# A decoder trunk in split fp32: in each weight tile, the products with the residual weights are moved behind all products with the rounded weights

## The chip, the cores and the metric

The kernel runs on one core of one Trainium2 chip. The metric is the device time of one execution in microseconds (us), as the median over several runs.

## The reference

Two decoder layers over 256 tokens of width 2048. Each layer has a token mixer (layer 0: forgetting attention "fox" with 16 heads of 128; layer 1: sliding-window attention "swa" with 32 query and 4 key heads of 64 and partial rotary) and a gated ConvFFN of width 5632. Everything is float32:

```python
for i in range(DEPTH):
    mod = c_act @ ada_w[i] + ada_b[i]            # six vectors of 2048 for this layer
    sh1, sc1, g1, sh2, sc2, g2 = jnp.split(mod[:, None, :], 6, axis=-1)
    h = x * (1.0 + sc1) + sh1
    y = fox_attention(h, ...) if i % 2 == 0 else swa_attention(h, positions, ...)
    x = layer_norm(DEEPNORM_ALPHA * x + (1.0 + g1) * y, ln_mix_g[i], ln_mix_b[i])
    h = x * (1.0 + sc2) + sh2
    y = conv_ffn(h, ...)                         # u = h @ w_up; conv of width 3; (silu(g) * val) @ w_down
    x = layer_norm(DEEPNORM_ALPHA * x + (1.0 + g2) * y, ln_ffn_g[i], ln_ffn_b[i])
```

## The kernel before

**Split products.** A float32 product is made of three matmuls in the type fp32r. Each operand is a rounded part (named H or h) and a residual, that is the operand less its rounded part (named L or l). Of the four products, residual times residual is left out. So each piece of weights costs rounded weights times rounded activations, rounded weights times residual activations, and residual weights times rounded activations.

**Weight tiles.** Weights pass through the chip once, in 728 tiles of 128 x 2 x 512 floats (two row blocks of 128, 512 columns, 512 KB). `stream` handles one tile: SP issues the DMA into `w` (a pool of 10 buffers that the tiles `wa` of the adaLN weights share), ScalarE (ACT) casts it to `wh` (line 259), VectorE (DVE) subtracts to get `wl` (line 270, called the residual cast below), and then TensorE (PE) runs the products. There are 4 buffers of `wh` and 4 of `wl`; a buffer is free when its last product has run.

**Two product loops.** `w_mm` keeps the weights stationary: 8 cells per tile (2 row blocks `i`, 4 column blocks `f`), each with a 128 x 256 output `ws`, two outputs to a PSUM bank; 24 matmuls a tile, 416 tiles (fox q and k, and both FFN up-projections). `x_mm` keeps the activations stationary and moves 512 weight columns: 4 cells (2 token halves `t`, 2 row blocks), outputs `xs` of one bank each; 12 matmuls a tile, 312 tiles (fox v, the swa input, both output projections, both FFN down-projections). `x_mm_end` is used for the last tiles of a stage: first all of them for `t=0`, then for `t=1`.

**Other work on the same engines.** The six adaLN vectors per layer are made on DVE in the background (`acc`, line 385, one instruction per 512 KB tile `wa`), at a rate per weight tile that is set stage by stage; in the opening (0 to about 174 us) the first two are made from tiles `wo` (`oacc`, lines 516 and 518) with PE sums `cps`. Attention heads run in steps between weight tiles: PE scores `S`, DVE and ACT softmax (`pr`, lines 633, 637, 645), PE transposes `T`, ACT copy `pT` (line 659), PE output `o`. `residual` (lines 561, 563, 565, 568) adds a finished stage to `x` and takes the LayerNorm moments, which GpSimd (POOL) turns into `rs`; then `normalise` (584, 586) and the transposes of `x` (463) make the next stage's `hH` and `hL`.

**What sets the order.** The program calls these in the order of the loops, but a scheduler of the framework orders the instructions of each engine from its own estimate of when operands are ready; instructions marked by `pin(..., True)` keep the program's order. Each engine then runs its list strictly in that order.

Of the kernel before, what the change touches and what calls it, by code (L numbers as in the profile page):

```python
# [17 lines left out]
P = 128  # L18
# [23 lines left out]
def hybrid_trunk(ctx: ExitStack, tc: tile.TileContext, a: dict, out: bass.AP):  # L42
# [32 lines left out]
    def mm(o, lhsT, rhs, start=False, stop=False, **kw):  # L75
        return nc.tensor.matmul(o, lhsT, rhs, start=start, stop=stop, **kw)  # L76
# [202 lines left out]
    def x_mm(ps, kc, h, l, stat, last, first=0, ts=range(NT)):  # L279

        for t in ts:
            for i in range(2):
                xh, xl = stat(kc + i, t)
                mm(ps[t], xh, h[:, i, :], start=kc + i == first)
                mm(ps[t], xh, l[:, i, :])
                mm(ps[t], xl, h[:, i, :], stop=kc + i == last)

    def x_mm_end(ps, stat, nk, n):

        kept = []  # L290

        def use(kc, h, l):
            end = kc >= nk - 2 * n
            x_mm(ps, kc, h, l, stat, nk - 1, ts=(0,) if end else range(NT))
            if end:
                kept.append((kc, h, l))
            if kc + 2 >= nk:
                for e in kept:
                    x_mm(ps, *e, stat, nk - 1, ts=(1,))

        return use

    def w_mm(ps, kc, h, l, last=KC - 1, first=0):

        for i in range(2):
            for f in range(4):
                o = ps[f // 2][:, f % 2, :]
                wh, wl = h[:, i, f * P:(f + 1) * P], l[:, i, f * P:(f + 1) * P]
                mm(o, wh, hH[:, kc + i, :], start=kc + i == first and f % 2 == 0, skip_group_check=True)
                mm(o, wh, hL[:, kc + i, :], skip_group_check=True)  # L310
                mm(o, wl, hH[:, kc + i, :], stop=kc + i == last, skip_group_check=True)

    def x_stationary(wsrc, col, k0, nk, stat, end=0):

        ps = x_banks()
        use = x_mm_end(ps, stat, nk, end) if end else lambda kc, h, l: x_mm(ps, kc, h, l, stat, nk - 1)
        stream(wsrc, k0, col, list(range(nk)), use)
        return ps

    def w_stationary(wsrc, col):  # L320

        ps = w_banks()
        stream(wsrc, 0, col, list(range(KC)), lambda kc, h, l: w_mm(ps, kc, h, l))
        return ps
# [127 lines left out]
    hH = cst.tile([P, KC, S], F32R, name="hH")  # L452
    hL = cst.tile([P, KC, S], F32R, name="hL")
# [248 lines left out]
    def fox(l, j):  # L702
# [118 lines left out]
        def first_block(blk, k2, part):  # L821
            if part == 0 and blk not in banks:
                def change():
                    for b, ps in banks.items():
                        if b not in old:
                            old[b] = []
                            for i, p in enumerate(ps):
                                g = [f32(gtile("part")).rearrange("p a b -> p (a b)") for _ in range(2)]
                                for gi, pi in zip(g, p):
                                    nc.scalar.copy(gi, pi if i == 2 else pi.rearrange("p a s -> p (a s)"))  # L830
                                old[b].append(g)
                    banks[blk] = w_banks(), w_banks(), x_banks()

                then(change)
            k = 2 * k2

            def use(kc, h, l):
                if part < 2:
                    w_mm(banks[blk][part], kc, h, l, last[blk])
                else:  # L840
                    x_mm(banks[blk][part], kc, h, l, hstat, last[blk])

            stream(w_in, 0, part * FW + blk * WB, [k, k + 1], use)
            done[blk] = k + 2
# [4 lines left out]
        for blk, rate in zip((1,0,2,3), (.9,1.1,1.2,1.4)):  # L849
            then(lambda rate=rate: ada.update(rate=rate))  # L850
            q, k, V = [], [], []
            n = done.get(blk, 0)

            def more(part, banks_, mul):
                if n == KC:
                    return banks[blk][part]
                ps = banks_()
                stream(w_in, 0, part * FW + blk * WB, list(range(n, KC)), lambda kc, h, l: mul(ps, kc, h, l, n))
                return ps

            o = old.get(blk, [None] * 3)
            wm = lambda ps, kc, h, l, n: w_mm(ps, kc, h, l, first=n)
            pq = more(0, w_banks, wm)
            then(lambda ps=pq, q=q, o=o: defer(evac_qk(ps, 0, q, o[0])))
            pk = more(1, w_banks, wm)
            then(lambda ps=pk, k=k, o=o: defer(evac_qk(ps, 1, k, o[1])))
            pv = more(2, x_banks, lambda ps, kc, h, l, n: x_mm(ps, kc, h, l, hstat, KC - 1, first=n))
            then(lambda ps=pv, V=V, o=o, hs=[head(blk, hh, q, k, V) for hh in range(4)]: defer(evac_v(ps, V, hs, o[2])))
# [229 lines left out]
```

## Time and profile before

| what | value |
|---|---|
| median of 3 runs | 2311.9 us (2309.21 to 2316.67) |
| profiled execution: span, the only time the page gives of it | 2317.4 us |
| PE busy / weight loads (PEld) busy | 97% / 89% |
| DVE / ACT busy | 78% / 49% |
| DMA, mean | 258 GB/s |
| residual casts, line 270 | 728, 1221 ns each |
| casts to rounded, line 259 | 728, 1051 ns each |
| adaLN accumulations, line 385 | 308, 1276 ns each |

The span runs from the first to the last instruction of one profiled execution. It is 5.5 us above the median of the runs, inside 0.3%. Ends of matmuls are modelled, so a busy PE only says that matmuls follow each other; their pace is read from how many start in a stretch. PEld is the weight load that precedes each matmul.

### The profile page before, as it was taken

Reading aid. Unit: us, or ns where it says so; the run is one execution under the profiler, and the core shown is the slowest. Engines: PE = TensorE matmul, PEld = TensorE weight load, DVE = VectorE, ACT = ScalarE, POOL = GpSimd, SP = SyncE. Lnnn points to the kernel's source line nnn. Section 1 sums busy time; section 2 is a strip of 40 time slices with the busy share of each in tenths; the row PEclk is TensorE's granted clock in tenths of the full one; section 3 lists DMA queues with packets and bytes.
Section 4 is the critical chain, followed back from the end, with each engine's and each line's share of the span. In section 5 each row is a group of like instructions: output and inputs, shape, how many; then the busy total and the mean of one; then the engine's idle time right before and its main releaser. Section 6 shows DMA issues by size and latency. Waiting matters only on the chain.

```text
span 2317.4 us, 38661 instructions
## 1 busy us (share of the span) xinstructions
PE 2243.1 (97%) x15061; PEld 2060.3 (89%) x15061; DVE 1804.0 (78%) x2609; ACT 1135.8 (49%) x1685; POOL 40.7 (2%) x79
## 2 busy tenths in 40 slices
PE   6899999999999999999999999999999999999997
PEld 5899998789999988999987778779999988999986
DVE  7788978879977876887887998899878655666655
ACT  1335654445555433454543478745555533454532
POOL 1001000010000000000001000000000000000000
PEclk9899999999999999999999999999999999999999
DMA  9998989968887897887897685778888566666663
GB/s 331 308 338 274 349 326 345 326 220 303 300 266 236 286 313 261 288 285 238 292 303 255 211 303 190 232 282 280 262 262 255 178 192 195 186 189 185 187 192 111
DMA packets 285561, 598.86 MB, mean 258 GB/s; under 512 B 20790, under 2 KB 53816, under 8 KB 285376
## 3 DMA queue, kind: packets, MB, share of 16 engines
q1 hardware_dynamic: 284768, 595.85, 78.1%
q8 instruction: 118, 1.93, 0.3%
q0 software_dynamic: 608, 0.53, 0.1%
q14 instruction: 67, 0.55, 0.1%
HBM read 594.21 MB, written 2.10 MB: 257 GB/s over the span
## 4 chain that ended last, share of the span: by engine, by line
PE 84%; DVE 10%; ACT 3%; issue 2%; DMA 1%; POOL 0%; SPq 0%; DVEq 0%; POOLq 0%; ACTq 0%
PE ws L76 49%; PE xs L76 30%; DVE wl L270 2%; DVE acc L385 2%; PE sm L76 1%; ACT wh L259 1%; PE cps L76 1%; PE o L76 1%; DVE oacc L518 1%; PE S L76 1%; PE sm L463 1%; ACT pr L645 0%; ACT pr L637 0%; PE T L657 0%; DVE x L563 0%
## 5 line engine op out<-in xcount | busy, mean ns | idle before, releaser
L270 DVE TENSOR_TENSOR wl<-w,wh 128x1024 fp32r<-128x1024 f32 x728 | 888.0, 1221 | 407.0 <-ACT wh L259 386.3
L259 ACT CAST wh<-w 128x1024 fp32r<-128x1024 f32 x728 | 762.9, 1051 | 864.6 <-PE ws L76 323.2
L76 PE MATMUL ws<-hH,wh 128*128 128x256 f32 x3328 | 945.8, 285 | 6.0 <-ACT wh L259 6.0
L76 PE MATMUL ws<-hH,wl 128*128 128x256 f32 x3328 | 936.9, 282 | 4.3 <-DVE wl L270 4.2
L76 PE MATMUL ws<-hL,wh 128*128 128x256 f32 x3328 | 939.5, 283 | 0.2 <-DVE hL L86 0.2
L76 PEld LDWEIGHTS ws<-hH,wh 128*128 128x128 f32 x3328 | 634.4, 191 | 10.0 <-ACT wh L259 6.8
L76 PEld LDWEIGHTS ws<-hH,wl 128*128 128x128 f32 x3328 | 637.2, 192 | 5.7 <-DVE wl L270 5.7
L76 PEld LDWEIGHTS ws<-hL,wh 128*128 128x128 f32 x3328 | 633.5, 190 | 2.7 <-issue 1.9
L76 PE MATMUL xs<-wh,gT 128*128 128x512 f32 x1408 | 437.2, 391 | 0.0
L385 DVE SCALAR_TENSOR_TENSOR acc<-wa,cact,acc 128x1024 f32<-128x1024 f32 x308 | 391.3, 1276 | 0.0
L76 PEld LDWEIGHTS xs<-wh,gT 128*128 128x128 f32 x1408 | 265.8, 189 | 55.4
L76 PE MATMUL xs<-wl,gT 128*128 128x512 f32 x704 | 275.1, 391 | 0.0
L76 PEld LDWEIGHTS xs<-wl,gT 128*128 128x128 f32 x704 | 133.0, 189 | 27.4
L76 PE MATMUL xs<-wl,hH 128*128 128x512 f32 x352 | 141.7, 403 | 5.5 <-DVE wl L270 5.5
L76 PE MATMUL xs<-wh,hL 128*128 128x512 f32 x352 | 140.8, 402 | 0.4 <-DVE hL L86 0.4
L76 PE MATMUL xs<-wh,hH 128*128 128x512 f32 x352 | 140.2, 408 | 0.2 <-ACT hH L473 0.2
L76 PE MATMUL xs<-wh,oT 128*128 128x512 f32 x384 | 125.4, 397 | 0.9 <-ACT pT L659 0.8
L987 ACT ACTIVATE u<-ws,ccol 128x256 f32<-128x256 f32 x176 | 96.5, 561 | 59.3 <-PE ws L76 52.0
L988 DVE SCALAR_TENSOR_TENSOR u<-ws,ccol,u 128x255 f32<-128x255 f32 x176 | 82.2, 476 | 20.5 <-ACT u L987 20.5
L76 PEld LDWEIGHTS xs<-wl,hH 128*128 128x128 f32 x352 | 67.8, 193 | 22.0 <-DVE wl L270 9.0
L76 PEld LDWEIGHTS xs<-wh,oT 128*128 128x128 f32 x384 | 72.8, 190 | 16.0 <-ACT pT L659 1.2
L990 DVE SCALAR_TENSOR_TENSOR u<-ws,ccol,u 128x254 f32<-128x254 f32 x176 | 83.1, 476 | 2.0
(211 smaller groups left out, 1564.4 us busy)
## 6 DMA issues: line engine op xcount, KB each, us to landing
w<-in_ffn_w_up_dram SPq DMA_DIRECT2D x352, 512.0 KB, 4.6
wa<-in_ada_w_dram SPq DMA_DIRECT2D x320, 512.0 KB, 5.1
w<-in_ffn_w_down_dram SPq DMA_DIRECT2D x176, 512.0 KB, 4.9
w<-in_fox_w_in_dram SPq DMA_DIRECT2D x96, 512.0 KB, 5.8
wo<-in_ada_w_dram SPq DMA_DIRECT2D x64, 512.0 KB, 6.5
w<-in_swa_w_in_dram SPq DMA_DIRECT2D x40, 512.0 KB, 4.9
w<-in_fox_w_o_dram SPq DMA_DIRECT2D x32, 512.0 KB, 6.3
w<-in_swa_w_o_dram SPq DMA_DIRECT2D x32, 512.0 KB, 5.5
```

The costliest lines, as they stand in the source:

```text
L76: return nc.tensor.matmul(o, lhsT, rhs, start=start, stop=stop, **kw)
L259: pin(nc.scalar.copy(h, w), False)
L270: pin(nc.vector.tensor_tensor(l, w, f32(h), op=ALU.subtract), False)
L385: pin(nc.vector.scalar_tensor_tensor(ac, wo, cact[:, k:k + 1], ac, op0=ALU.mult, op1=ALU.add), True)
L463: nc.tensor.transpose(o[:, t * P:(t + 1) * P], x[:, t, (k + j) * P:(k + j + 1) * P], ident)
L518: nc.vector.scalar_tensor_tensor(acc[:, v, k % 2, :], w[:, k, :], cact[:, kc:kc + 1], acc[:, v, k % 2, :], op0=ALU.mult, op1=ALU.add)
L987: nc.scalar.activation(u, pf, AF.Identity, bias=cw(CW, f), scale=cw(2, f))
L988: nc.vector.scalar_tensor_tensor(u[:, 1:], pf[:, :S - 1], cw(1, f), u[:, 1:], op0=ALU.mult, op1=ALU.add)
L990: nc.vector.scalar_tensor_tensor(u[:, 2:], pf[:, :S - 2], cw(0, f), u[:, 2:], op0=ALU.mult, op1=ALU.add)
```

## The change

In both loops the matmuls that read `wl` are moved behind all matmuls of the same tile that read `wh`. Number, shapes and operands of the matmuls stay as they are; the accumulation into each output has another order. The start flag stays with the first product, the stop flag moves to the last residual product of the cell.

```diff
 def x_mm(...):
         for t in ts:
             for i in range(2):
                 xh, xl = stat(kc + i, t)
                 mm(ps[t], xh, h[:, i, :], start=kc + i == first)
-                mm(ps[t], xh, l[:, i, :])
-                mm(ps[t], xl, h[:, i, :], stop=kc + i == last)
+                mm(ps[t], xl, h[:, i, :])
+        for t in ts:
+            for i in range(2):
+                mm(ps[t], stat(kc + i, t)[0], l[:, i, :], stop=kc + i == last)
...
 def w_mm(...):
-        for i in range(2):
-            for f in range(4):
-                o = ps[f // 2][:, f % 2, :]
-                wh, wl = h[:, i, f * P:(f + 1) * P], l[:, i, f * P:(f + 1) * P]
-                mm(o, wh, hH[:, kc + i, :], start=kc + i == first and f % 2 == 0, skip_group_check=True)
-                mm(o, wh, hL[:, kc + i, :], skip_group_check=True)
-                mm(o, wl, hH[:, kc + i, :], stop=kc + i == last, skip_group_check=True)
+        cells = [(i, f, ps[f // 2][:, f % 2, :]) for i in range(2) for f in range(4)]
+        for i, f, o in cells:
+            wh = h[:, i, f * P:(f + 1) * P]
+            mm(o, wh, hH[:, kc + i, :], start=kc + i == first and f % 2 == 0, skip_group_check=True)
+            mm(o, wh, hL[:, kc + i, :], skip_group_check=True)
+        for i, f, o in cells:
+            mm(o, l[:, i, f * P:(f + 1) * P], hH[:, kc + i, :], stop=kc + i == last, skip_group_check=True)
```

The scheduler makes another list of it, on PE and, by its estimates, on DVE and ACT too; the lists of SP and POOL hold the same instructions in the same order. Lines below the edit are numbered two higher in the changed kernel.

On PE, one weight tile of the fox output projection (`wh_4718` and `wl_4719` are its two parts, `oT` the heads' outputs in rounded and residual form, `xs_4636` and `xs_4637` the two token halves). Before:

```order
L76 MATMUL xs_4636<-wh_4718,oT_2521 128x512
L76 MATMUL xs_4637<-wh_4718,oT_2521 128x512
L76 MATMUL xs_4636<-wl_4719,oT_2521 128x512
L76 MATMUL xs_4636<-wh_4718,oT_2521 128x512
L76 MATMUL xs_4636<-wh_4718,oT_2565 128x512
L76 MATMUL xs_4636<-wl_4719,oT_2565 128x512
L76 MATMUL xs_4636<-wh_4718,oT_2565 128x512
L76 MATMUL xs_4637<-wl_4719,oT_2521 128x512
```

The same tile on PE after the change:

```order
L76 MATMUL xs_4636<-wh_4718,oT_2521 128x512 x2
L76 MATMUL xs_4636<-wh_4718,oT_2565 128x512 x2
L76 MATMUL xs_4637<-wh_4718,oT_2521 128x512 x2
L76 MATMUL xs_4637<-wh_4718,oT_2565 128x512 x2
L76 MATMUL xs_4636<-wl_4719,oT_2521 128x512
L76 MATMUL xs_4636<-wl_4719,oT_2565 128x512
L76 MATMUL xs_4637<-wl_4719,oT_2521 128x512
L76 MATMUL xs_4637<-wl_4719,oT_2565 128x512
```

The first matmul that reads `wl` stood third (the scheduler had already put one other in front of it) and now stands ninth of twelve.

On DVE, the LayerNorm between the first FFN and swa (`t_13239` and `t_13250` are the two token halves of the last residual, `mv` their moments, `wl_13237` and `wl_13321` residual casts of tiles of the next stage). Before:

```order
L561 TENSOR_TENSOR t_13239<-xs_12961,gate_7333 128x512
L563 TENSOR_TENSOR x_108<-x_108,t_13239 128x512
L565 BN_STATS stats_128<-x_108 128x6
L561 TENSOR_TENSOR t_13250<-xs_12962,gate_7333 128x512
L568 BN_AGGR mv_13243<-stats_128 128x2
L270 TENSOR_TENSOR wl_13237<-w_13234,wh_13236 128x1024
L563 TENSOR_TENSOR x_108<-x_108,t_13250 128x512
L270 TENSOR_TENSOR wl_13321<-w_13318,wh_13320 128x1024
```

The same stretch on DVE after the change:

```order
L563 TENSOR_TENSOR t_13239<-xs_12961,gate_7333 128x512
L565 TENSOR_TENSOR x_108<-x_108,t_13239 128x512
L567 BN_STATS stats_128<-x_108 128x6
L270 TENSOR_TENSOR wl_13237<-w_13234,wh_13236 128x1024
L570 BN_AGGR mv_13243<-stats_128 128x2
L563 TENSOR_TENSOR t_13250<-xs_12962,gate_7333 128x512
L270 TENSOR_TENSOR wl_13321<-w_13318,wh_13320 128x1024
L565 TENSOR_TENSOR x_108<-x_108,t_13250 128x512
```

One residual cast has moved ahead of the moments of the first token half. The LayerNorm before the first FFN shows the same move; at the one before the second FFN a cast stood ahead of the moments already.

On ACT, in the attention of fox (`pr_2297` and `pr_2345` are the probabilities of two heads, line 637 their exponentials, 645 their scaling). Before:

```order
L259 CAST wh_2356<-w_2354 128x1024
L637 ACTIVATE pr_2297,ss_2298<-pr_2297,nm_2296 128x128
L637 ACTIVATE pr_2297,ss_2298<-pr_2297,nm_2296 128x256
L259 CAST wh_2393<-w_2391 128x1024
L645 ACTIVATE pr_2297<-pr_2297,ss_2298 128x128
L645 ACTIVATE pr_2297<-pr_2297,ss_2298 128x256
L659 COPY pT_2342<-T_2338 128x384
```

The same stretch on ACT after the change:

```order
L259 CAST wh_2356<-w_2354 128x1024
L259 CAST wh_2393<-w_2391 128x1024
L639 ACTIVATE pr_2297,ss_2298<-pr_2297,nm_2296 128x128
L639 ACTIVATE pr_2297,ss_2298<-pr_2297,nm_2296 128x256
L661 COPY pT_2342<-T_2338 128x384
L647 ACTIVATE pr_2297<-pr_2297,ss_2298 128x128
L647 ACTIVATE pr_2297<-pr_2297,ss_2298 128x256
```

A cast of weights has moved ahead of a head's exponentials; in the swa attention some casts have moved the other way, behind the work of two or three heads.

## The prediction

> **What bounds the kernel now.** I read the page first, then the table of stages, then who waits for whom, then single stretches. The page gives the span, the busy engines and the chain that ended last.
>
> ```profile
> span 2317.4 us, 38661 instructions
> PE 2243.1 (97%) x15061; PEld 2060.3 (89%) x15061; DVE 1804.0 (78%) x2609; ACT 1135.8 (49%) x1685; POOL 40.7 (2%) x79
> PE ws L76 49%; PE xs L76 30%; DVE wl L270 2%; DVE acc L385 2%; PE sm L76 1%; ACT wh L259 1%; PE cps L76 1%; PE o L76 1%; DVE oacc L518 1%; PE S L76 1%; PE sm L463 1%; ACT pr L645 0%; ACT pr L637 0%; PE T L657 0%; DVE x L563 0%
> ```
>
> PE's products are 79% of the chain, the residual cast only 2%. So PE sets the time nearly everywhere, and what the change can win is what PE waits for `wl`. The waits, whole span, PE and its weight loads:
>
> ```profile
> PE xs L76 <- DVE wl L270: 12.4, 11, 2.3
> PE ws L76 <- DVE wl L270: 4.2, 4, 1.7
> PEld xs L76 <- DVE wl L270: 19.2, 18, 2.7
> PEld ws L76 <- DVE wl L270: 5.7, 6, 1.9
> ```
>
> These are the same waits seen twice: 16.6 us before matmuls (too little, since a matmul's modelled end runs into the wait), 24.9 us before weight loads (too much, since a load is idle for part of each matmul anyway). Less than 1.1% of the span is at stake. The same view cut into stretches, in order 100 to 174, 430 to 470 (two rows), 470 to 1300, 1300 to 1400 and 1400 to 1560 us; between 174 and 430 and after 1560 it has no row of PE for `wl`:
>
> ```profile
> PE ws L76 <- DVE wl L270: 2.1, 2, 1.4
> PE xs L76 <- DVE wl L270: 6.3, 4, 2.3
> PEld xs L76 <- DVE wl L270: 8.3, 5, 2.7
> PE ws L76 <- DVE wl L270: 0.4, 1, 0.4
> PE xs L76 <- DVE wl L270: 3.8, 4, 1.6
> PE xs L76 <- DVE wl L270: 0.6, 1, 0.6
> ```
>
> That is 13.2 us; the remaining 3.4 lie before 100 us. Now each stretch, with PE, PEld, DVE, ACT and POOL busy, clock, DMA share and GB/s:
>
> ```profile
> 58.00:116.00 58.00, 50.75 (x314) 46.60 (x313) 44.63 (x96) 20.64 (x26) 0.00 (x0) 0.85 0.94 308
> 116.00:174.00 58.00, 55.90 (x424) 52.72 (x423) 47.20 (x96) 18.27 (x20) 0.00 (x0) 1.00 0.99 338
> 442.00:466.00 24.00, 17.73 (x74) 13.08 (x73) 23.97 (x26) 6.42 (x7) 0.00 (x0) 1.00 0.90 307
> 470.00:500.00 30.00, 30.00 (x139) 24.90 (x138) 19.72 (x22) 11.34 (x11) 1.03 (x1) 1.00 0.79 264
> 1318.00:1360.00 42.00, 38.22 (x186) 30.39 (x185) 40.43 (x74) 24.47 (x45) 0.00 (x0) 1.00 0.90 309
> 1490.00:1546.00 56.00, 55.22 (x247) 44.27 (x246) 52.73 (x65) 24.90 (x38) 0.00 (x0) 1.00 0.83 290
> 1975.00:2190.00 215.00, 215.00 (x1828) 1.00 0.64 187
> 2200.00:2290.00 90.00, 90.00 (x399) 1.00 0.57 175
> ```
>
> The opening is at the limit of the DMAs, the fox output projection (442 to 466) at that of DVE, which has 0.03 us idle in 24; swa is nearly so (40.43 of 42), and the FFNs are pure PE (last two rows, PE alone: 1828 matmuls of `w_mm` in 215 us, 399 of `x_mm` in 90).
>
> **The change part by part.** Nothing is added or removed; `wl` is wanted later in its tile by about 7 of 12 matmuls of 0.226 us in `x_mm` (last row above: 90 / 399), so by 1.6 us, and by 14 of 24 in `w_mm`. SP's and POOL's lists stay.
>
> *Fox output projection, -2.4.* PE and DVE side by side (start, length, count, idle before):
>
> ```profile
> 456.95 0.84 PE L76 MATMUL xs<-wh,oT 128*128 128x512 f32 x3
> 460.10 0.50 PE L76 MATMUL xs<-wl,oT 128*128 128x512 f32 x1 [2.31 <-DVE wl L270]
> 462.27 0.84 PE L76 MATMUL xs<-wh,oT 128*128 128x512 f32 x3
> 464.94 0.50 PE L76 MATMUL xs<-wl,oT 128*128 128x512 f32 x1 [1.83 <-DVE wl L270]
> 456.45 2.46 DVE L385 SCALAR_TENSOR_TENSOR acc<-wa,cact,acc 128x1024 f32<-128x1024 f32 x2
> 458.84 1.21 DVE L270 TENSOR_TENSOR wl<-w,wh 128x1024 fp32r<-128x1024 f32 x1
> 461.29 2.46 DVE L385 SCALAR_TENSOR_TENSOR acc<-wa,cact,acc 128x1024 f32<-128x1024 f32 x2
> 463.67 1.22 DVE L270 TENSOR_TENSOR wl<-w,wh 128x1024 fp32r<-128x1024 f32 x1
> ```
>
> Each residual cast comes after two accumulations and other work, and DVE never rests. PE in the new order runs its 8 `wh` products meanwhile, but then waits for the same cast: DVE's list of work is as long as before. What counts is the last cast that binds, at 463.67; after it PE has 1.6 us less to do. So of 6.3 us I take 1.6, not the 6.3 of a wait that simply vanishes. The wait has a second price:
>
> ```profile
> 466.50:470.00 3.50, 3.50 (x10) 2.70 (x9) 3.50 (x4) 1.04 (x1) 0.00 (x0) 0.55 0.98 338
> 470.00:473.50 3.50, 3.50 (x17) 2.86 (x16) 2.37 (x3) 1.05 (x1) 0.00 (x0) 1.00 1.05 403
> ```
>
> Right behind it the granted clock is 0.55 and 10 matmuls start where 17 do next: about 7 x 0.21 = 1.5 us. Shorter waits remain in the new order, so I take half, 0.8 (bounds 0 and 1.5).
>
> *Opening, -1.0.* With DMAs at 0.94 to 0.99 a PE that gets ahead waits for the next tile instead; of the 3.4 us before 100 us nothing, of the 2.1 behind it half (bounds 0 and 2.1).
>
> *470 to 1300, -0.4*: a single wait, in a stage where DVE has slack after 466. *swa, -2.0*: DVE has 1.57 us idle in 42, so at least the 1.6 of the last binding cast and at most the 3.8; near the first, as DVE is 96% busy. *1400 to 1560, 0*: DVE has no gap from 1500 to 1546 (casts for the next stage among it) and the LayerNorm behind it waits for DVE, not PE. Gains: 2.4 + 1.0 + 0.4 + 2.0 = 5.8.
>
> *Other target at each matmul, +2.7.* The steady FFN stretch, by form:
>
> ```profile
> L76 PE MATMUL ws<-hH,wl 128*128 128x256 f32 x610 | 171.5, 281 | 0.0
> L76 PE MATMUL ws<-hL,wh 128*128 128x256 f32 x609 | 171.2, 281 | 0.0
> L76 PE MATMUL ws<-hH,wh 128*128 128x256 f32 x609 | 171.2, 281 | 0.0
> ```
>
> 215 / 1828 = 117.6 ns from start to start. Sorted by what follows what, the starts of these 1828 rows lie 118.3 ns apart where the next matmul goes to another cell's output (from `hH,wl` to `hH,wh`) and 117.5 where it adds to the same output. Before, 8 of 24 steps change the output; now 8 in the `wh` pass and 8 in the `wl` pass: 8 more of 0.8 ns in 416 tiles, 3328 x 0.8 = 2.7 us. No row shows residual products one after the other; the bounds are 0 (it is the reload, not the output) and 3328 x 1.4 = 4.7, from the lowest and highest mean of the 24 positions of a tile (117.2 and 118.6). I take the middle since the output is what those steps share. [...]
>
> *LayerNorm, +1.0.* A residual cast of 1.22 us stands ahead of the first half's moments at two more places. There PE waits already:
>
> ```profile
> PE sm L463 <- ACT x L584: 6.8, 3, 5.0
> PE sm L463 <- DVE x L586: 4.3, 2, 2.3
> ```
>
> The ACT wait (5.0 of it before swa) hangs on those moments, so a cast there can cost its 1.2; the DVE waits hang on the second half, which follows anyway. The `wh` buffer before it comes free two matmuls earlier, which gives 0.45 back. I take 0.7 before swa, 0 before the first FFN (the second half ends later there) and 0.3 before the second FFN; bounds -0.5 and 2.4.
>
> Sum against the profiled execution: -5.8 + 2.7 + 1.0 = -2.1, span 2317.4 to 2315.3. The median is 5.5 lower: 2311.9 - 2.1 = 2309.8 us, -0.1%. A measurement of this kernel tells about 0.3%, 6.9 us, from no change.
>
> **The rivals.**
>
> *The waits really vanish (faster).* ACT's casts start earlier (a `wh` buffer is free 8 or 4 matmuls before its tile ends), so DVE gets at its casts earlier and each waits out behind 8 products. Then all 13.2 us and the 1.5 of the clock go: -14.7 + 3.7 = -11.0, 2301; with the larger PEld numbers (8.3 for 6.3) a few us more, to 2296. For it: no wait is longer than 2.7 us. Against: DVE at 23.97 of 24.
>
> *Attention on ACT (slower).* The scheduler now puts casts of 1.05 us ahead of softmax steps. ACT's casts and the waits for softmax:
>
> ```profile
> L259 ACT CAST wh<-w 128x1024 fp32r<-128x1024 f32 x728 | 762.9, 1051 | 864.6 <-PE ws L76 323.2
> PE qp L936 <- ACT pT L659: 1.6, 2, 0.9
> PE T L657 <- ACT pr L645: 1.2, 1, 1.2
> PE xs L76 <- ACT pT L659: 0.8, 1, 0.8
> ```
>
> One head held up by one cast costs PE 1.05; there are 48 heads. 9 heads decide (9.0 us are needed to turn -2.1 into +6.9); 12 would give -2.1 + 12.6, 2322. Against: PE now waits 3.6 us in all for softmax, and between a head's scores and its transposes stand as many matmuls as before.
>
> *A change of output costs more.* At 3.5 ns a change (11.7 us / 3328) the whole is slower by 0.3%; only steps of up to 1.4 ns are seen.
>
> *The clock falls.* If changing the output at each matmul made PE pause enough to halve the clock in the `wl` pass, 416 x 8 x 0.118 = 393 us would be added: 2705. The granted clock is 1.00 over 215 us in which every third matmul changes it. [...]
>
> *It doesn't do what it says.* The new list has `wl` last, so PE's order does change; but where DVE sends its casts later by as much, nothing is won: +3.7, 2315.6, within 0.3%.
>
> **How the numbers follow.** Forecast (2305 to 2318.8) 0.50; waits vanish 0.28; ACT 0.10; dearer output 0.05; clock 0.02; nothing won 0.05. Faster is 0.28; same 0.50 + 0.05 = 0.55; slower 0.17. The range reaches over the first rival's 2296 and the second's 2322 and leaves out the dearer tails, under 2 in 10; the forecast's own range is 2303 to 2316 (gains 14.7 to 3.6, costs 0 to 7.1, not all at one end).
>
> **What would show it.** PE's waits for `wl`: near 5 us in 430 to 470 and 2 in 1300 to 1400, 0 to 1 elsewhere. DVE still gapless in 442 to 466. The last FFN's matmuls 117.9 ns apart instead of 117.6. The ACT wait at the transposes of `x` about 1 us longer. I am wrong if waits for `wl` are gone altogether, if PE waits for softmax reach 10 us, or if the FFN pace moves by over 1 ns.

## The result, and the profile after

| kernel | median, us | runs | ratio to before (95% interval) |
|---|---|---|---|
| before | 2311.8 | 20 | |
| changed | 2301.8 | 20 | 0.9957 (0.9945 to 0.997) |

The changed kernel is faster by 0.43%, 10.0 us; predicted were 2.1. So 2301.8 lies below the 2303 to 2316 that the forecast gave itself, and at the 2301 of its first rival. (One of the twelve executions of the kernel of experiment 3 took 10397 us; it is left out of the ratio given there.) The profiled execution of the changed kernel has a span of 2301.2 us. The page, in the places that were read before:

```profile
span 2301.2 us, 38651 instructions
PE 2231.3 (97%) x15061; PEld 2051.1 (89%) x15061; DVE 1799.2 (78%) x2609; ACT 1129.5 (49%) x1685; POOL 38.6 (2%) x79
PE ws L76 50%; PE xs L76 32%; DVE wl L270 2%; DVE acc L387 1%; PE sm L76 1%; DVE oacc L520 1%; ACT wh L259 1%; PE cps L76 1%; PE S L76 1%; PE o L76 1%; PE sm L465 1%; PE T L659 0%; ACT pr L639 0%; ACT pr L647 0%; DVE x L565 0%
```

The chain has the same shape, with products at 82% in place of 79%. The waits, whole span (total, times, longest), with the one for `wh` beside them; before, that one was 6.0:

```profile
PEld xs L76 <- DVE wl L270: 9.0, 6, 2.7
PE xs L76 <- DVE wl L270: 6.5, 5, 2.3
PEld ws L76 <- DVE wl L270: 1.4, 2, 1.1
PE ws L76 <- DVE wl L270: 0.9, 1, 0.9
PE ws L76 <- ACT wh L259: 8.1, 4, 2.3
```

PE's waits for `wl` fell from 16.6 to 7.4 us, and 2.1 came back as waits for `wh`. Where they stand, with PE's other waits before products there: two rows from 420 to 470 us and two from 1290 to 1400. The remaining 0.9 lie before 100 us:

```profile
PE xs L76 <- DVE wl L270: 4.6, 3, 2.3
PE xs L76 <- DVE hL L86: 1.4, 1, 1.4
PE xs L76 <- DVE wl L270: 2.0, 2, 1.6
PE xs L76 <- ACT wh L259: 1.1, 1, 1.1
```

The table of stages, its windows shifted with the work from 436 us on:

```profile
58.00:116.00 58.00, 52.76 (x362) 48.51 (x362) 50.39 (x108) 21.53 (x27) 0.00 (x0) 0.94 1.01 343
116.00:174.00 58.00, 55.81 (x409) 52.64 (x408) 45.68 (x90) 22.30 (x25) 4.83 (x7) 0.97 0.97 333
436.00:460.00 24.00, 19.42 (x83) 15.06 (x82) 23.96 (x27) 7.03 (x8) 0.00 (x0) 1.00 0.90 303
460.90:464.30 3.40, 3.40 (x10) 2.63 (x9) 3.40 (x4) 0.41 (x1) 0.00 (x0) 0.50 0.94 284
464.30:467.70 3.40, 3.40 (x16) 2.79 (x16) 3.23 (x3) 1.44 (x2) 0.00 (x0) 1.00 1.04 379
1311.00:1353.00 42.00, 38.15 (x185) 30.56 (x184) 40.46 (x75) 24.41 (x45) 0.00 (x0) 1.00 0.88 316
1600.00:1700.00 100.00, 100.00 (x884) 100.00 (x884) 85.68 (x115) 54.22 (x75) 0.00 (x0) 1.00 0.87 290
1959.00:2174.00 215.00, 215.00 (x1828) 215.00 (x1827) 133.62 (x180) 108.53 (x149) 0.00 (x0) 1.00 0.64 187
```

Two rows are not as expected. From 58 to 116 us PE starts 362 matmuls where it started 314, the clock is 0.94 for 0.85, and the DMAs move 343 GB/s for 308. And the second FFN from 1600 to 1700 us, where PE waits for nothing, starts 884; the kernel before, in the same 100 us:

```profile
1600.00:1700.00 100.00, 100.00 (x852) 100.00 (x851) 82.47 (x108) 52.83 (x73) 0.00 (x0) 1.00 0.84 277
```

The last FFN stretch (1959 to 2174, the second half of the second FFN's up-projection; "last FFN" below) has the same 1828 in 215 us as before. To see where the 16.2 us between the two spans arise, count the products of `w_mm` and `x_mm` from the program's start, 13728 in all, and compare when the same one starts. The changed kernel is ahead by 7.0 us at the end of the opening (the 720th), 5.5 where the fox output projection begins (2040th), 6.8 at its end, 5.8 in the first FFN and up to the LayerNorm before swa, 8.4 at the end of swa, 8.3 some tiles into the second FFN; then it gains 0.5 us with every 120 products until 1780 us, 16.2 in all, and nothing after.

**Two paces.** By the steps between starts, `w_mm` runs either 117.8 or 113.3 ns from start to start, in gapless stretches of up to 1920 matmuls. Before has both; from 1080 to 1140 us its matmuls read 276 ns where the steady stretch of the prediction has 281:

```profile
L76 PE MATMUL ws<-hH,wh 128*128 128x256 f32 x178 | 49.1, 276 | 0.0
L76 PE MATMUL ws<-hH,wl 128*128 128x256 f32 x177 | 48.9, 276 | 0.0
```

So 7.9 us of the 16.2 may have nothing to do with the order of products. The experiments had to part the two.

### The profile page after: what moved, and what is told of

It reads as the page before. It is cut to its first block, busy times and chain, and to the rows that moved or that the text cites. A ratio compares the mean times of both kernels' runs of the same rounds, so it can differ in the third digit from the quotient of the medians.

```text
span 2301.2 us, 38651 instructions
## 1 busy us (share of the span) xinstructions
PE 2231.3 (97%) x15061; PEld 2051.1 (89%) x15061; DVE 1799.2 (78%) x2609; ACT 1129.5 (49%) x1685; POOL 38.6 (2%) x79
## 4 chain that ended last, share of the span: by engine, by line
PE 87%; DVE 8%; ACT 3%; issue 2%; DMA 1%; POOL 0%; SPq 0%; DVEq 0%; POOLq 0%; ACTq 0%
PE ws L76 50%; PE xs L76 32%; DVE wl L270 2%; DVE acc L387 1%; PE sm L76 1%; DVE oacc L520 1%; ACT wh L259 1%; PE cps L76 1%; PE S L76 1%; PE o L76 1%; PE sm L465 1%; PE T L659 0%; ACT pr L639 0%; ACT pr L647 0%; DVE x L565 0%
## 5 line engine op out<-in xcount | busy, mean ns | idle before, releaser
L76 PE MATMUL ws<-hH,wh 128*128 128x256 f32 x3328 | 808.8, 284 | 8.1 <-ACT wh L259 8.1
L76 PE MATMUL ws<-hL,wh 128*128 128x256 f32 x3328 | 802.5, 282 | 0.5 <-DVE hL L86 0.4
L76 PE MATMUL ws<-hH,wl 128*128 128x256 f32 x3328 | 457.7, 280 | 1.0 <-DVE wl L270 0.9
L76 PEld LDWEIGHTS ws<-hH,wl 128*128 128x128 f32 x3328 | 419.2, 189 | 1.4 <-DVE wl L270 1.4
L76 PE MATMUL xs<-wh,gT 128*128 128x512 f32 x1408 | 351.5, 391 | 0.0
L76 PE MATMUL xs<-wl,gT 128*128 128x512 f32 x704 | 189.9, 390 | 0.0
L76 PE MATMUL xs<-wl,hH 128*128 128x512 f32 x352 | 98.7, 399 | 2.0 <-DVE wl L270 2.0
L76 PE MATMUL xs<-wh,oT 128*128 128x512 f32 x384 | 99.4, 398 | 0.0
```

## The experiments

Opening here means the start of the 720th product; old and new are the two orders.

**1. The kernel before, profiled again.**

> The kernel before, unchanged, profiled a second time, to tell what belongs to the order of the products and what to the single execution. In the two profiles at hand the matmuls of w_mm run gapless at one of two paces, 117.8 or 113.3 ns from start to start, for up to 2000 matmuls on end; the first half of the second FFN has 117.8 before and 113.3 after, worth 1784 x 4.45 ns = 7.9 us of the 16.2 us between the spans. Theory 1 (the pace is set by the instant at which PE's last wait ends, not by the order of products): this profile may show either pace in that stretch and again 113.3 in the second half of the first FFN's up-projection, and the opening up to 170 us is within 2 us of the first profile. Theory 2 (the old order is what makes it 117.8): 117.8 there again. Rival for the opening: if its length differs here by 5 us or more from the first profile, the 7 us that the opening gave are chance too.

Span 2314.9, opening 188.1 us (first profile 187.2). The first FFN from 580 to 680 us, first and second profile of this kernel (PE alone, then all engines):

```profile
580.00:680.00 100.00, 100.00 (x852) 1.00 0.87 290
```

```profile
580.00:680.00 100.00, 100.00 (x885) 100.00 (x884) 89.49 (x115) 55.02 (x78) 0.00 (x0) 1.00 0.88 300
```

The same program ran one stretch at either pace. The second FFN was at 117.8 again, which fits both theories; the half behind 1061 us, "again 113.3" by theory 1, was at 117.8, so that expectation missed: this stretch takes either pace too.

**2. One loop alone.** In the first kernel only `w_mm` has the new order, in the second only `x_mm`:

```diff
 # kernel 1: as in the change
-        for i in range(2):
-            for f in range(4):
+        cells = [(i, f, ps[f // 2][:, f % 2, :]) for i in range(2) for f in range(4)]
...
 # kernel 2: as in the change
-                mm(ps[t], xh, l[:, i, :])
-                mm(ps[t], xl, h[:, i, :], stop=kc + i == last)
+                mm(ps[t], xl, h[:, i, :])
...
```

> The new order in w_mm alone, x_mm as before. Theory of the prediction: w_mm only loses by it (+2.7 for the change of output, +0 to 1 at the LayerNorms, -0.5 for w tiles in the opening), about +2.5 us, ratio 1.001. Rival (outputs cost nothing; the gain is in waits and in the half-clock phases that follow them): the waits at 31.4 and 86.8 us of the opening, both before ws matmuls, go, with half of the half-clock phases there, -2 to -4 us, ratio 0.998 to 0.999; the waits of the fox output projection (6.3 us) and of swa (3.8) stay.

> The new order in x_mm alone, w_mm as before. Theory of the prediction: -2.4 in the fox output projection, -0.4, -2.0 in swa, -0.5 in the opening, up to +1 at the LayerNorms, together -4.5 to -5.3 us, ratio 0.998. Rival: the two waits before xs matmuls in the opening (61.8 and 82.4 us, 1.0 us each) take the half-clock phases at 63 to 77 us with them, and with what the changed kernel's profile shows behind 420 us (fox output projection -1.2, swa -1.8) it is -5 to -8 us, ratio 0.9965 to 0.998.

`w_mm` alone: 2303.7 us, ratio 0.9977 (0.9959 to 0.9995); `x_mm` alone: 2305.5, 0.9976 (0.9958 to 0.9995). Each brings about 0.23%. The prediction had `w_mm` losing 2.5 us, and that expectation missed. The waits of the fox output projection, 420 to 470 us, `w_mm` alone and then `x_mm` alone:

```profile
PE xs L76 <- DVE wl L270: 6.3, 4, 2.3
```

```profile
PE xs L76 <- DVE wl L270: 3.6, 4, 2.3
```

The opening ended at 181.0 us with `w_mm` alone and at 184.0 with `x_mm` alone.

**3. The opening alone.** A flag `late` chooses the order and is turned once the opening's tiles are issued:

```diff
+    late = [True]
...
+        if late[0]:
...          (the loop in the new order)
+        else:
...          (the loop in the old order)
         opening(plan, first_block)
         settle()
+        late[0] = not late[0]
```

> The new order, both loops, in the opening alone (the tiles whose products are issued up to about 170 us); everything behind it in the old order. Theory of the prediction: -1.0 us (half of 2.1 behind 100 us; nothing before it, because the DMAs were taken to be at their limit), ratio 0.9996. Rival: the opening gives the larger half of the gain, -6 to -7 us as between the two profiles (PE reaches 170 us that much earlier, DMA in 58 to 116 us moves 340 GB/s in place of 308, and the granted clock there is 0.94 in place of 0.85), ratio 0.997.

The profile shows the opening at 180.9 us, 6 us shorter, but the ratio is 1.0005 (0.999 to 1.002): nothing. In that profile the up-projection of the first FFN ran at 117.8 from 523 us on. Either the opening's gain is lost later, or the paces that these runs met hid it; the median alone can't tell. The pace had to be taken out.

**4. Holding the pace.** Over the first six profiles I sorted what had last interrupted the stream of `w_mm` matmuls, and the pace behind it. After an output product of a fox head (fp32, 256 and 128 columns) it was 113.3 ns 36 times of 36; after one fp32 product of 512 columns, as the gate sums are, 117.8 ns 48 times of 48; after the eight products of a head's scores it changed over each time, 54 of 54. So two fp32 products were put at seven places of the up-projections, into a bank that nobody reads:

```diff
+PIN = ((4, 9), (5,))
...
+    def extra(h):
+
+        d = bank("du")
+        mm(d[:, :S], ones, f32(h[:, 0, :S]), start=True, stop=True, skip_group_check=True)
+        mm(d[:, S:S + P], ones, f32(h[:, 1, :P]), start=True, stop=True, skip_group_check=True)
...
-    def w_stationary(wsrc, col):
+    def w_stationary(wsrc, col, at=None):
...
+        def use(kc, h, l):
+            if kc == at:
+                extra(h)
+            w_mm(ps, kc, h, l)
...
-                ps = w_stationary(w_up, b * WB)
+                ps = w_stationary(w_up, b * WB, {1: 8, 6: 2}.get(b))
...
-                ps = w_stationary(w_up, DFF + b * WB)
+                ps = w_stationary(w_up, DFF + b * WB, 2 if b in PIN[l] else None)
```

> The kernel before, with two more fp32 matmuls (ones by 256 and by 128 columns of a wh tile, into a bank that nobody reads) at seven places of the FFN up-projections: early in the first half of each up-projection, in its fifth block, early in the second half, and in the fourth block of the second half in layer 0. In the profiles so far every group of that shape (the output products o of the fox heads, 4 records of 215, 215, 108 and 31 ns) is followed by the pace of 113.3 ns, 36 times of 36; a single fp32 matmul of 512 columns (the gate sums) by 117.8, 48 of 48. Theory 1 (the pace is set by the last thing that interrupted the stream of w_mm): all long stretches of the FFNs run at 113.3; against the first profile some 1094 + 600 + 1140 + 1790 + 400 + 1900 = 6900 matmuls gain 4.45 ns each, 31 us, less 7 x 0.66 = 4.6 us for the insertions: -20 to -26 us against the runs, whose stretches are partly at 113.3 already, ratio 0.989 to 0.992. Theory 2 (the pace is chance or set by something else): stretches of both paces, +4.6 us, ratio 1.002.

> The changed kernel with the same seven insertions. Theory 1 (the pace is set by what interrupts the stream, and the order of products changes waits only): all long stretches at 113.3 ns here too, and the difference to the old order with insertions is what the order is worth without the pace: -8 us (7 in the opening, 1.2 in the fox output projection, 1.8 in swa, less about 2 lost elsewhere), ratio to before about 0.987. Rival (most of the measured 10 us is a pace that the new order meets more often): less than 4 us between the two kernels with insertions. Theory of the prediction (a change of output costs 0.8 ns): the FFN stretches of this kernel are slower by 0.1 to 0.4 ns a matmul than those of the old order with insertions.

Old order 2289.1 us, ratio 0.9904 (0.9878 to 0.9929); new order 2286.6, 0.9896 (0.9868 to 0.9923). Two FFN stretches of the new order with insertions:

```profile
1620.00:1720.00 100.00, 100.00 (x885) 100.00 (x884) 79.62 (x103) 52.98 (x72) 0.00 (x0) 1.00 0.82 273
1980.00:2080.00 100.00, 100.00 (x885) 100.00 (x884) 67.73 (x97) 54.27 (x76) 0.00 (x0) 1.00 0.62 194
```

The last FFN, at 117.8 in all six earlier profiles, is at 113.3 as well, in both kernels. Fourteen small matmuls bring the old order 22 us here (by the ratio) and 14 in the repeat below, and the new one 15 (2301.8 to 2286.6). Between the orders only 2.5 us are left, less than the 4 that the rival named.

**5. The four combinations under one pace.** Both orders once more, and the new order in the opening only or behind it only, all with the insertions (the edits are those of 3 and 4; `late` starts as `False` for the second):

> The new order in the opening alone, with the seven insertions that hold the FFNs at 113.3 ns. Theory 1 (the opening gives most of what the order is worth, and the first measurement of it, 1.0005, was the pace met elsewhere in those runs): -5 to -6 us against the old order with insertions (2289), so 2283 to 2284, as the profiles have it: PE reaches the end of the opening at 180 to 181 us in three of three with the new order in it, 185 to 188 in three of three with the old. Theory 2 (what the opening gains is lost again later, or shows in the profiled execution only): 0 to -1.5, 2287.5 to 2289.

> The old order in the opening, the new one in everything behind it, with the seven insertions. Theory 1: only what PE waits for wl in the fox output projection and in swa, -1.2 and -1.8, less what the waits for wh and for softmax take back, so -1 to -3 us against the old order with insertions, 2286 to 2288. Theory of the prediction: -2.4 - 0.4 - 2.0 + 2.7 + 1.0 = -1.1, 2288.

> The old order with the seven insertions once more, beside the two kernels above. 2286 to 2292 again, and the opening at 185 to 188 us in its profile; theory 2 above: the opening varies with the execution and is as short as 181 here.

> The new order with the seven insertions once more. Theory 1: 5 to 8 us below the old order with insertions of this call, about 2283. Rival (the pace made most of the measured 10 us): 2.5 us below, as the first two medians were apart (2289.1 and 2286.6).

| opening | behind it | median, us | mean, us | ratio to before (95% interval) |
|---|---|---|---|---|
| old | old | 2290.3 | 2290.6 | 0.9938 (0.9917 to 0.9958) |
| new | old | 2284.5 | 2285.6 | 0.9916 (0.9896 to 0.9936) |
| old | new | 2289.8 | 2289.1 | 0.9927 (0.9904 to 0.9949) |
| new | new | 2285.3 | 2284.6 | 0.9911 (0.9889 to 0.9934) |

By means of six runs each the opening brings 5.0 us, the rest 1.5, both 6.0; with experiment 4 (2.5) both bring 4.2, give or take 2.6 (95%, from the scatter of the 24 runs). With the new order behind it the opening brings 4.5 us, so on average 4.8, give or take 2.6. So the opening does gain, though experiment 3 did not show it (the paces of its runs are known for the profiled one only); the rest can't be told from nothing by times. But the opening also varies by itself. From 58 to 116 us: old behind new, new, then the two repeats, old and new:

```profile
58.00:116.00 58.00, 50.64 (x313) 46.29 (x311) 44.41 (x96) 20.52 (x26) 0.00 (x0) 0.85 0.95 305
```

```profile
58.00:116.00 58.00, 52.84 (x363) 48.55 (x362) 50.75 (x108) 21.52 (x27) 0.00 (x0) 0.94 1.01 345
```

```profile
58.00:116.00 58.00, 50.49 (x347) 46.35 (x347) 47.18 (x102) 20.68 (x26) 0.00 (x0) 0.94 0.96 319
```

```profile
58.00:116.00 58.00, 52.76 (x347) 48.94 (x346) 49.76 (x107) 21.62 (x27) 0.00 (x0) 0.88 0.99 338
```

(The first row is the kernel with the old order in the opening and the new one behind it.) With the old order the clock was once 0.94, with the new one once 0.88, and both then start 347 matmuls; so theory 2 of the repeat, an old opening as short as 181, nearly came true (182.4).

**6. The changed kernel again, and the other insertion.** The second kernel has `extra` with one fp32 product of 512 columns at the same seven places:

```diff
-        mm(d[:, :S], ones, f32(h[:, 0, :S]), start=True, stop=True, skip_group_check=True)
-        mm(d[:, S:S + P], ones, f32(h[:, 1, :P]), start=True, stop=True, skip_group_check=True)
+        mm(d, ones, f32(h[:, 0, :]), start=True, stop=True, skip_group_check=True)
```

> The changed kernel once more, without insertions. Theory 1 (the order is worth 4 to 6 us, nearly all in the opening, and the rest of the first 10 us is the pace that the FFN stretches happened to meet): -4 to -10 us against before, depending on how often each meets 113.3 ns; in the profile the opening ends near 181 us (179 to 185 in the five profiles with the new order there), the stretch of the first FFN behind 700 us and the second half of the second FFN run at 117.8, and the two stretches that took either pace so far (530 to 700 us and 1575 to 1780 us) take either. Theory 2 (the new order itself brings 113.3 in the second FFN): 113.3 again in 1575 to 1780 us.

> The changed kernel with seven insertions at the same places, but each is one fp32 matmul of 512 columns (ones by a wh tile, 0.52 us), the shape after which w_mm ran at 117.8 ns 48 times of 48. Theory 1 (what interrupts the stream sets the pace of the hundreds of matmuls behind it): all long stretches at 117.8; some 7200 matmuls of 4.45 ns more than with the other insertion, 32 us, less 7 x 0.14: about 2285 + 31 = 2316, ratio to before 1.002 to 1.004, and 12 to 15 us above the changed kernel without insertions. Theory 2 (any insertion lets PE fall into the faster pace, or the pace is chance): below 2300.

The changed kernel: 2300.4 us, 0.9973 (0.9951 to 0.9994); its second FFN was at 113.3 again, and so was the first up to 693 us, but not the half behind 1061. The other insertion: 2320.0 us, 1.0034 (1.0016 to 1.0052), and the two stretches of experiment 4:

```profile
1620.00:1720.00 100.00, 100.00 (x852) 100.00 (x851) 79.76 (x104) 52.52 (x75) 0.00 (x0) 1.00 0.79 260
1980.00:2080.00 100.00, 100.00 (x852) 100.00 (x851) 65.18 (x92) 52.23 (x75) 0.00 (x0) 1.00 0.59 186
```

The same kernel is 34 us apart with the one insertion and the other (2286.6 and 2285.3 against 2320.0; 32 were worked out). In the profiles, all seven insertions of two products are followed by 113.3 in each of the six profiles that have them, and all seven of one product by 117.8. That the interrupting matmul sets the pace of hundreds behind it is thereby shown; which of its properties does it is not, as the two insertions differ in number, columns and length. The new order with the first insertion is the version that beats both kernels: 1.0% below before, where the change alone is 0.3 to 0.4% below.

## Why the prediction was right and wrong

All 14 profiles sorted by the order at each place (length of the stretch from the starts of the same products, means of four to seven profiles; kernels with both orders at a place are left out there, and the row of the fox attention has only the kernels with one order throughout):

| place (products) | old, us | new, us | difference | predicted |
|---|---|---|---|---|
| opening, to the 720th | 186.1 (182.4 to 188.1) | 180.6 (179.2 to 184.6) | -5.5 | -1.0 |
| fox attention, 720 to 1920 | 206.5 | 208.0 | +1.5 | 0 |
| fox output projection, 2040 to 2280 | 67.8 (67.3 to 68.1) | 66.4 (66.0 to 66.9) | -1.4 | -2.4 |
| LayerNorm before swa, 7440 to 7680 | 72.9 (71.4 to 73.4) | 71.6 (70.8 to 73.2) | -1.3 | +0.7 |
| swa with the waits for `wl`, 7680 to 8040 | 122.4 | 122.4 | 0.0 | -2.0 |
| swa behind them, 8040 to 8400 | 113.6 | 112.7 | -1.0 | 0 |
| the two other LayerNorms | | | -0.1, +0.1 | 0, +0.3 |
| change of output in `w_mm` | 117.8 or 113.3 ns | 117.8 or 113.3 ns | 0 | +2.7 |

**The opening was mis-sized, and its reason was wrong.** "With DMAs at 0.94 to 0.99 a PE that gets ahead waits for the next tile instead": from 58 to 116 us the DMAs went from a share of 0.94 and 308 GB/s to 1.01 and 343, so they had been held back. PE's waits for `wl` in the opening fell from 5.6 to 0.9 us, those for `wh` rose by 2.1, which leaves 2.6. The second part is the clock, whose row (0.85) stood in the prediction but was priced only behind the fox output projection. By the granted clock's records the first 180 us hold 27.3, 27.3, 23.9, 17.1 and 27.3 us at half clock in the five old openings, and 17.1 four times, 20.5 twice and 27.3 once in the seven new ones. At equal half-clock time the new order is about 3 us shorter (182.4 against 179.2 to 180.2 at 17.1; 187.2 to 188.1 against 184.6 at 27.3, so with a single opening on one side each time), and 10.2 us more of it cost 5 us in either order. On average the new openings have 5.1 us less, worth 2.5: together 5.5. The new order with insertions, run twice, had the same waits in both openings and 20.5 and 27.3 us of half clock, so the half clock behind the same waits differed between the two executions. All half-clock phases of the openings last 3.4, 6.8 or 10.2 us: 10.2, 3.4, 6.8, 3.4 and 3.4 in the first profile of the kernel before, 6.8, 6.8 and 3.4 in the first of the changed one.

**The output projection: right mechanism. Swa: the waits fell, the time did not.** PE's waits were forecast as near 5 and 2 us and came as 4.6 and 2.0, the single one of 0.4 between 470 and 1300 us is gone, and DVE is as gapless (23.96 of 24). The binding casts of the output projection in the profile after (DVE and PE's weight loads in turn):

```profile
453.38 1.23 DVE L270 TENSOR_TENSOR wl<-w,wh 128x1024 fp32r<-128x1024 f32 x1
454.66 0.77 PEld L76 LDWEIGHTS xs<-wl,oT 128*128 128x128 f32 x4 [2.73 <-DVE wl L270]
458.24 1.22 DVE L270 TENSOR_TENSOR wl<-w,wh 128x1024 fp32r<-128x1024 f32 x1
459.51 0.77 PEld L76 LDWEIGHTS xs<-wl,oT 128*128 128x128 f32 x4 [2.22 <-DVE wl L270]
```

All 8 products with `wh` are through, and PE still waits for the same cast; what is saved is the work behind the last one. The measured 1.4 is near the 1.6 of that step. The 0.8 for half of the clock's price did not come in this profile: the row at 460.9 has 0.50 and as many matmuls as before. Over all profiles the half-clock phase is missing in two of the seven with the new order there and in none of the seven with the old.

In swa the waits for `wl` fell as forecast, from 3.8 to 2.0 us, but beside the 1.1 for `wh` above two more rows from 1290 to 1400 us are new:

```profile
PE qp L938 <- DVE qq L930: 0.7, 1, 0.7
PE T L659 <- ACT pr L647: 0.4, 1, 0.4
```

From the 7680th to the 8040th product (1301 to 1423 us before) all waits of PE together are 4.7 us with the old order and 4.3 to 4.4 with the new, and the stretch takes 122.4 us in all 14 profiles. So the step that took at least the 1.6 us behind the last binding cast failed here: PE met other waits instead. That swa and the LayerNorm before it together still gained (-2.2, with -1.3 forecast) is luck: 1.3 came at the LayerNorm, where a loss of 0.7 was forecast, and 1.0 behind 1423 us, where nothing was.

**The output price does not exist.** The last FFN runs 1828 matmuls in 215 us in either order, though every `wl` product now changes its output. The 0.8 ns between steps was a pattern inside one pace, taken for a price of what the steps share: in the changed kernel's last FFN still every third step has 118.3 ns and the others 117.5, whether the output changes there or not. The lower bound, 0, was the value. Nor did the clock fall where every `wl` product changes the output: it is 1.00 over those 215 us.

**LayerNorm: the costs did not come.** The waits at the transposes of `x`, whole span:

```profile
PE sm L465 <- ACT x L586: 6.0, 2, 4.0
PE sm L465 <- DVE x L588: 3.6, 3, 2.0
```

Before the second FFN PE waits 2.0 us for ACT (0.9 before) and 1.0 for DVE (2.0 before), the same in all. Before swa it waits 4.0 for ACT (5.0 before) and 0.5 for DVE, in all seven profiles with the new order in `x_mm` alike, and there the stage is 1.3 us shorter; the half clock in it is 10.2 us in five of these seven and 13.6 in six of the seven with the old order. Why ACT comes a microsecond earlier although a cast stands ahead of the moments was not tried.

**The fox attention: a term that the sum did not have.** The softmax rival is seen in small: the one wait for a head's probabilities (near 230 us) is 1.0 to 1.2 us with the old order throughout and 1.5 to 1.7 with the new one throughout, far from 10. The 1.5 us of the table lie elsewhere. The last 60 products, 1860 to 1920, take 18.9 us in the four kernels with the old order throughout and 20.5 to 20.6 in all ten others, also in the two that have the old order there and the new one in the opening alone. At that place stand 32 one-column matmuls (the adaLN sums, last section), and the clock falls to half for 3.4 us in the four kernels and for 6.8 in the ten. In the kernels with the new order only in `x_mm` or only behind the opening, one more half-clock phase follows the wait near 230 us, and their fox attention is 3.3 to 3.8 us longer.

**What the sum misses.** The differences add to -7.6 us (before rounding), the runs under one pace to -4.2 (give or take 2.6): 1 us stays unexplained between them. The change itself was measured twice, at 9.9 and 6.2 us by the ratios 0.9957 and 0.9973. What lies between 4.2 and these may be the pace of the second FFN's first half. It was at 113.3 in seven of seven profiles with the new order in `w_mm` there and in three of seven with the old; 1790 matmuls by 4.45 ns are 8.0 us, by 4/7 more often 4.5 us. The first FFN took 113.3 four times of seven with either order. That the order makes 113.3 likelier there is a count, noticed after the fact, and not shown: by chance alone such a split comes about 1 time in 29. So the forecast had the direction, and a size that was off by the opening and the change of output, by half-clock phases, and by a pace that it did not know; the rival that gave 2301 had the number without its reason, for the waits did not vanish.

## What to carry to other kernels

A wait that shrinks has gained what the stage gains between the same two products: in swa the waits for `wl` fell by 1.8 us and the stage by nothing. Price a short wait of PE with the half clock that can follow it (here 0.50 for 3.4 us behind the output projection, with 10 matmuls started where 16 start next), in every stage where the granted clock is below 1.00, and take a DMA share of 0.94 as a limit only if the GB/s equal the best stretch of the same kernel (here 308 became 343). Before a difference between two profiles is explained, profile one of the kernels twice and count the matmuls that start in 100 gapless microseconds: a change of pace between executions can be larger than the edit (here 852 or 885 from the same kernel, 8.0 us over 1790 matmuls, where the edit was worth 4.2). Where such a stream settles at the longer step, a small neutral matmul after the last interruption is worth a trial; which shape works has to be measured (here 113.3 ns followed one of the two tried, 117.8 the other).

## What the runs showed of the hardware that was not expected

At full clock, products with 256 moving columns settled at 113.3 or 117.8 ns from start to start and held it for up to 1920 matmuls; those with 512 columns had one pace, 226.7, in the four stretches of 348 to 576 that the first profile of either kernel has. Behind the opening, a stretch of `w_mm` that follows `x_mm` directly ran at 117.8 in 18 of 18 cases of the first six profiles; in the opening, with the stretch that begins at its end, it went over to 113.3 within ten matmuls in 24 of 30 (stretches of ten and more). No run tells what in PE keeps the pace.

The clock fell during one-column matmuls. In the kernel before, 32 of them (the adaLN sums, 112 ns from start to start at full clock, 213 at half) run gapless from 1057.6 us, and the clock falls during them without any wait (PE alone, before):

```profile
1056.80:1060.20 3.40, 3.40 (x33) 1.00 0.59 186
1060.20:1063.60 3.40, 3.40 (x18) 0.50 0.63 184
1063.60:1067.00 3.40, 3.40 (x17) 0.50 0.04 15
```

Each profile has four such groups with no wait of PE beside them; in 51 of the 56 the clock falls to half during the group or within 1.6 us of its last matmul, for 3.4 or 6.8 us.
